# Recurrence gates from stacked high and low parts, and PSUM banks in rings of five and three

## The chip, the cores and the metric

The kernel runs on one core of one Trainium2 chip. The metric is the device time of one execution in microseconds, as the median of several runs. Below, PE is the matrix engine (TensorE), PEld its weight loads, DVE is VectorE, ACT is ScalarE, POOL is GpSimd and SP is the engine that issues most DMA transfers. A PE product writes into PSUM, which has eight banks; ACT and DVE read the results there.

## The reference, cut to what matters

The reference is one layer of a decoder that takes 1024 prompt tokens and 8 single tokens of other sequences, 1032 columns in all, through the same weights, in float32:

```python
z = x @ w_in                                     # one projection, 7680 columns for all branches
xr, yr, q, k, v, xq, g = split(z)
xc = conv4(xr);  a_out = rg_lru(xc) * gelu(yr)   # branch A
s_out = window_attention(q, k, v)                # branch B
c_out = memory_attention(xq, mem_k, mem_v)       # branch C
merged = sum(sigmoid(g[n] + b[n]) * (branch[n] @ w_branch[n]) for n in range(3))
h = layer_norm(ALPHA * x + merged @ w_out)
y = layer_norm(ALPHA * h + (silu(gate) * up) @ w_down)     # gate, up = split(h @ w_gate_up)
```

Inside `rg_lru` stand two small products, which the change is about. The 1024 channels are 16 blocks of 64, and each block has its own 64x64 matrix for each of two gates:

```python
r = sigmoid(einsum('btni,nij->btnj', xblk, wa) + ba)
i = sigmoid(einsum('btni,nij->btnj', xblk, wx) + bx)
log_a = -8 * r * softplus(-lam);  a = exp(log_a)
u = sqrt(-expm1(2 * log_a)) * (i * xf)           # then h = a * h + u along time
```

## The kernel before, in words

**Precision.** Each float32 operand is split into a high part, a cast to a shorter format made by ACT (L76), and a low part, the rest, made by a DVE subtraction (L77). A product is then three matmuls into one PSUM bank: high x high, high x low and low x high. `mm3` (L117 to L119) issues them.

**Recursive products.** Most large products are not multiplied block by block. `fast_step` computes a pair of 128-row output tiles ("a unit") from a 2x2 partition with seven products instead of eight, each from sums of quarters of the weights (`fast_quarter`) and of the input (`combos`, `h_combos`). A unit has seven steps, i = 0 to 6. Each step runs over two column halves, p = 0 and 1, of 258 columns, with twelve matmuls each (L237 to L239). Steps 0, 2, 4 and 6 add into one bank per half (`ub`), steps 1 and 5 into another (`ud`), step 3 has its own (`uc`). ACT copies the bank out after step 0 (`p1s`), step 1 (`p5s`) and step 2 (`u2s`), at L263; DVE reads it after step 3 (`za`, L265), step 4 (`zb`, L267) and step 5 (`za`, L270); ACT reads it after step 6 (`zb`, L1648). Within one bank the next step that adds must wait until the read before it is over: step 2 for p1s, step 4 for u2s, step 6 for zb of step 4. The quarters of the weights are cut three steps ahead.

**Stages.** `project` begins with the keys and values of the memory (`mem_kv`), then runs 30 units for the input projection. Behind each of its steps `pump` lets one side job issue a piece of work: the recurrence (`lru`) of a channel tile, the memory attention of the eight single tokens (`dec_mem`, whose dot products run on DVE from caches fetched by DMA, L895 and L901), or the transposed values. Then come the attentions, mixed with the branch products `bra`, `brc`, `brs`; the output projection; the gate and up products and most of the down products, again as recursive units (`gate_up_down`); and the last products (`dl`).

**Gates of the recurrence.** `lru(m)` works on tile m, that is 128 channels or two blocks of 64. The two 64x64 matrices of a gate stand on the diagonal of a 128x128 matrix that is otherwise zero, so `wr` is 128x256: gate a, then gate x. The columns are done in three thirds of 344. In each, xc is split into `xch` and `xcl`, and for each gate `mm3` makes three matmuls into the bank `g`, from which ACT writes the tanh of all 128 rows (L829) into `tr` (gate a) and `ti` (gate x). One piece of this is issued behind a step of the current unit.

**PSUM.** One pool of eight banks serves the whole kernel, in rings by use: `mm` 3, `s` 2, `t` 2, `o` 1. In `fast_step` the first sum takes from `mm`, the second from `t`, step 3 from `s`. The gates, the transposes of the single tokens (`drt_c`, `dct`) and the transposed values share the one bank of `o`.

**Order.** Up to the first six steps the order on every engine is as written. After that a scheduler places the instructions of each queue; PE keeps the order of the program but for small transposes, while ACT, DVE and SP get another order when costs or dependencies change. Each queue runs strictly in its order.

Of the kernel before, what the change touches and what calls it, by code (L numbers as in the profile page):

```python
# [10 lines left out]
F32 = mybir.dt.float32  # L11
# [7 lines left out]
P = 128  # L19
# [7 lines left out]
NM = 256  # L27
# [31 lines left out]
class Builder:  # L59
# [84 lines left out]
    def setup(self):  # L144
        nc, ctx, tc, io = self.nc, self.ctx, self.tc, self.io
        self.cst = ctx.enter_context(tc.tile_pool(name="cst", bufs=1))
        self.psum = ctx.enter_context(tc.tile_pool(name="psum", bufs=1, space=PSUM))
# [81 lines left out]
    def fast_product(self, st, i, p, ts, ps, opens):  # L229
# [5 lines left out]
        for k in range(4):  # L235
# [2 lines left out]
            mm(sh[:, w], xl, start=False, stop=False)  # L238
            self.last_mm = mm(sl[:, w], xh, start=False, stop=k == 3).ins  # L239

    def fast_step(self, st, i, ts, finish):

        nc, u, scale = self.nc, st["u"], getattr(finish, "scale", 1.0)
        cols = lambda th, p: slice(HT * th + QN * p, HT * th + QN * (p + 1))
        small = lambda tag, p: self.w1.tile([P, QN], F32, tag=tag, name=f"{tag}{u}_{p}", bufs=2)
        if i == 3:
            st["za"] = self.zt(f"za{u}")
        if i == 4:
            st["zb"] = self.zt(f"zb{u}")
        for p in range(2):  # L250
            if i == 0:
                st["b", p] = self.bank("mm", f"ub{u}_{p}")[:, :QN]
            elif i == 1:
                st["d", p] = self.bank("t", f"ud{u}_{p}")[:, :QN]
            elif i == 3:
                st["c", p] = self.bank("s", f"uc{u}_{p}")[:, :QN]
            b, c, d = st.get(("b", p)), st.get(("c", p)), st.get(("d", p))
            ps = {0: b, 1: d, 2: b, 3: c, 4: b, 5: d, 6: b}[i]
            self.fast_product(st, i, p, ts, ps, i in (0, 1, 3))
            add = partial(nc.vector.scalar_tensor_tensor, scalar=scale, op0=ALU.mult, op1=ALU.add)  # L260
            if i in (0, 1, 2):
                st["s", i, p] = small(("p1s", "p5s", "u2s")[i], p)
                self.last_copy = nc.scalar.mul(st["s", i, p], ps, scale).ins  # L263
            elif i == 3:
                add(st["za"][:, cols(0, p)], c, in1=st["s", 0, p])  # L265
            elif i == 4:
                self.last_evac = nc.vector.scalar_tensor_tensor(st["zb"][:, cols(1, p)], b, -scale, st["s", 1, p],  # L267
                                                                op0=ALU.mult, op1=ALU.subtract).ins
            elif i == 5:
                add(st["za"][:, cols(1, p)], d, in1=st["s", 2, p])  # L270
# [119 lines left out]
    def mem_kv(self, moving, xs, load, quarters):  # L390
# [7 lines left out]
        def put(ps, name, m):  # L398
            raw = self.ph.tile([P, 256], F32, tag="kvraw", name=f"{name}r{m}", bufs=4)
            nc.scalar.copy(raw, ps)  # L400
            nc.gpsimd.dma_start(self.scr[name][:, m, :], raw)

        def mem_raw(k):
# [20 lines left out]
        def key(n):  # L424
            m, e = n // 2, n % 2
            if e == 0:
                sums[m] = self.bank("mm", f"mk{m}")[:, :NM]
            hi, lo = pairs.pop(n)
            cols = [slice(i * P, (i + 1) * P) for i in range(4)]
            self.mm3(sums[m], [((hi[:, w], lo[:, w]), memx[4 * e + i]) for i, w in enumerate(cols)], e == 1, e == 0)  # L430

        def value(n):
            g, j = (n - 16) // 4, n % 4
            if j == 0:
                sums[g] = [self.bank("mm", f"mv{g}_{tt}")[:, :256] for tt in range(2)]
            hi, lo = pairs.pop(n)
            cols = [slice(i * 256, (i + 1) * 256) for i in range(2)]
            for tt in range(2):
                xs_ = [tuple(a[:, tt * P:(tt + 1) * P] for a in memx[2 * j + i]) for i in range(2)]
                self.mm3(sums[g][tt], [(x, (hi[:, w], lo[:, w])) for x, w in zip(xs_, cols)], j == 3, j == 0)  # L440

        warm = self.bank("o", "warm")
        for _ in range(WARM):
# [306 lines left out]
    def lru_consts(self):  # L750
# [9 lines left out]
        self.hbg = self.cst.tile([P, 24], F32, name="hbg")  # L760
        nc.vector.tensor_scalar_mul(self.hbg, self.vec[:, V_BG:V_BG + 24], 0.5)
# [38 lines left out]
    def lru(self, m, xr, yr):  # L800
# [15 lines left out]
        nc.gpsimd.tensor_copy(self.pconv[:, m, :], xr[:, TP - 3:TP])  # L816
        nc.gpsimd.tensor_copy(self.scvo[:, m, 0:2, :], buf[:, 1:3, :])
        nc.gpsimd.tensor_copy(self.scvo[:, m, 2, :], xr[:, TP:T])
        wgh, wgl = (self.lr.tile([P, 256], F32R, tag=f"wg{e}", name=f"wg{e}{m}", bufs=1) for e in "hl")
        self.split(wgh, wgl, wr)  # L820
        a, ti = self.zt(f"tr{m}"), self.zt(f"ti{m}")
        for c, (t0, n) in enumerate(THIRDS):
            xch, xcl = (self.lr.tile([P, n], F32R, tag=f"xc{e}", name=f"xc{e}{m}_{c}", bufs=1) for e in "hl")
            self.split(xch, xcl, xc[:, t0:t0 + n])
            yield
            for j, (dst, hb) in enumerate(((a, self.hba), (ti, self.hbx))):
                ps = self.bank("o", f"g{m}_{j}_{c}")[:, :n]
                self.mm3(ps, [((wgh[:, j * P:(j + 1) * P], wgl[:, j * P:(j + 1) * P]), (xch, xcl))])
                nc.scalar.activation(dst[:, t0:t0 + n], ps, AF.Tanh, bias=hb[:, m:m + 1], scale=0.5)  # L829
                yield  # L830

        sp2, sp4n = self.sp2[:, m:m + 1], self.sp4n[:, m:m + 1]
# [698 lines left out]
    def build(self):  # L1531
# [9 lines left out]
        self.wpool = self.ctx.enter_context(pool("wpool"))  # L1541
        self.ctx.enter_context(pool("edge", "right")).tile([P, 8], F32, name="edge")
        self.zbufs = 9
        with pool("tp", "right") as self.tp, pool("w1") as self.w1, pool("z") as self.z, ExitStack() as late:
            self.project(late, pool)
        self.act, self.merged, self.first_gates = {}, {}, []
        with ExitStack() as right:
            slots = right.enter_context(ExitStack())
# [36 lines left out]
            with pool("zf") as self.z:  # L1585
                with ExitStack() as tx:
                    self.g, self.wl, self.wraw, self.A = [], [], [], {}
                    with pool("lnp") as self.ph:
# [5 lines left out]
                    with pool("w1") as self.w1:  # L1594
# [94 lines left out]
def _pack(i):  # L1689
# [28 lines left out]
    blk = np.zeros((KT, P, 256), np.float32)  # L1718
    for j, name in enumerate(("lru_wa", "lru_wx")):
        w = f[name][0].reshape(KT, 2, 64, 64)  # L1720
        for e in range(2):
            blk[:, e * 64:(e + 1) * 64, j * P + e * 64:j * P + (e + 1) * 64] = w[:, e]
    o["wlru"] = blk
# [53 lines left out]
```

## Time and profile before

| | us |
|---|---|
| median of 3 runs | 1907.44 (1907.36 to 1909.93) |
| the profiled execution | 1909.41 |
| its span, first to last instruction | 1907.6 |
| PE busy in the span | 1889.4 |
| DVE busy | 1389.9 |
| ACT busy | 1014.8 |

The profile shows one execution. PE matmuls are pipelined: one starts while the one before still runs, so its busy time says that PE had work, and its rate is read from the spacing of starts. A row of a group gives line, engine, operation, what it writes and reads, how often; then the busy time, the mean duration in ns, the idle time before it, and what ended that. A row of the timeline gives start, duration, engine, line, operation. The chain of waits is followed back from the last instruction. The mean granted clock of PE was 0.997.

### The profile page before, as it was taken

What the parts mean: (1) busy time and instruction counts of PE and PEld (TensorE: products, weight loads), DVE (VectorE), ACT (ScalarE), POOL (GpSimd) and SP (SyncE); (2) the same over time, 40 slices, a digit from 0 to 9 for tenths busy, and PEclk for the clock granted to TensorE, in tenths of its full rate; (3) what the DMA queues carried; (4) which work ended last, traced back from release to release, by engine and by line L of the source; (5) the groups of instructions that cost most, each with busy time, mean ns of one, the idle gap of its engine ahead of it and who ended that gap; (6) DMA issues with size and microseconds to landing.
All of it is one profiled execution on the core that took longest, in us unless ns stands there. A gap on an engine that the chain in (4) does not pass through costs nothing.

```text
span 1907.6 us, 38153 instructions
## 1 busy us (share of the span) xinstructions
PE 1889.4 (99%) x14878; PEld 1870.0 (98%) x14878; DVE 1389.9 (73%) x2712; ACT 1014.8 (53%) x2124; POOL 112.8 (6%) x190
## 2 busy tenths in 40 slices
PE   9999999999999999999999999999999999999998
PEld 8999999999999999999999999999999999999997
DVE  7868877977887657578887467786666667858486
ACT  6555564555665656578775234543433433636354
POOL 1000000010000000022210000000000000001200
PEclk9999999999999999999999999999999999999998
DMA  8535434546444368546435351133355335759872
GB/s 316 171 119 173 136 128 139 172 144 214 136 150 147 113 209 264 181 144 208 144 100 164 111 190 51 57 122 118 111 165 191 106 123 177 269 127 272 174 211 90
DMA packets 175973, 302.18 MB, mean 158 GB/s; under 512 B 18912, under 2 KB 92592, under 8 KB 175792
## 3 DMA queue, kind: packets, MB, share of 16 engines
q1 hardware_dynamic: 169120, 280.64, 45.0%
q0 software_dynamic: 4224, 14.78, 3.9%
q10 hardware_dynamic: 2448, 4.33, 0.6%
q8 instruction: 116, 1.90, 0.4%
q14 instruction: 65, 0.53, 0.1%
HBM read 217.97 MB, written 85.89 MB: 159 GB/s over the span
## 4 chain that ended last, share of the span: by engine, by line
PE 90%; DMA 4%; DVE 3%; ACT 2%; issue 1%; SPq 0%; DVEq 0%; ACTq 0%
PE ub L237 5%; PE ub L239 5%; PE ub L238 5%; PE ubfg L238 4%; PE ubfg L237 4%; PE ubfg L239 4%; PE ud L239 3%; PE ud L237 3%; PE ud L238 3%; PE udfg L237 2%; PE udfg L238 2%; PE udfg L239 2%; PE ubf L237 2%; PE op L117 2%; PE ubf L238 2%; PE ubf L239 2%
## 5 line engine op out<-in xcount | busy, mean ns | idle before, releaser
L645 ACT ACTIVATE bp<-bp,bst 128x257 f32<-128x257 f32 (+1 forms) x128 | 62.8, 493 | 38.5 <-DVE bst L639 37.8
L237 PE MATMUL ub<-th,u_0h 128*128 128x258 f32 x240 | 68.6, 286 | 1.0 <-ACT zb L1648 1.0
L237 PE MATMUL ub<-th,u_6h 128*128 128x258 f32 x240 | 68.7, 286 | 0.0
L237 PE MATMUL ub<-th,u_4h 128*128 128x258 f32 x240 | 68.0, 283 | 0.7 <-ACT u2s L263 0.7
L237 PE MATMUL ub<-th,u_2h 128*128 128x258 f32 x240 | 68.0, 283 | 0.4 <-ACT p1s L263 0.4
L239 PE MATMUL ub<-th,u_0l 128*128 128x258 f32 x240 | 68.0, 283 | 0.0
L639 DVE CUSTOM_DVE_ANT_0 bp<-bs,mask,nsnk 128x256 f32<-128x256 f32 (+1 forms) x128 | 55.8, 461 | 16.8 <-PE bs L636 16.4
L239 PE MATMUL ud<-th,u_5l 128*128 128x258 f32 x240 | 68.0, 283 | 0.0
L237 PE MATMUL ud<-th,u_5h 128*128 128x258 f32 x240 | 67.9, 283 | 0.0
L239 PE MATMUL ud<-th,u_1l 128*128 128x258 f32 x240 | 67.9, 283 | 0.0
L239 PE MATMUL ub<-th,u_2l 128*128 128x258 f32 x240 | 67.9, 283 | 0.0
L239 PE MATMUL uc<-th,u_3l 128*128 128x258 f32 x240 | 67.9, 283 | 0.0
L239 PE MATMUL ub<-th,u_6l 128*128 128x258 f32 x240 | 67.9, 283 | 0.0
L239 PE MATMUL ub<-th,u_4l 128*128 128x258 f32 x240 | 67.9, 283 | 0.0
L237 PE MATMUL uc<-th,u_3h 128*128 128x258 f32 x240 | 67.9, 283 | 0.0
L237 PE MATMUL ud<-th,u_1h 128*128 128x258 f32 x240 | 67.9, 283 | 0.0
L238 PE MATMUL ub<-tl,u_0h 128*128 128x258 f32 x240 | 67.6, 282 | 0.0
L238 PE MATMUL ub<-tl,u_6h 128*128 128x258 f32 x240 | 67.5, 281 | 0.0
L238 PE MATMUL ub<-tl,u_2h 128*128 128x258 f32 x240 | 67.4, 281 | 0.0
L238 PE MATMUL uc<-tl,u_3h 128*128 128x258 f32 x240 | 67.4, 281 | 0.0
L238 PE MATMUL ud<-tl,u_5h 128*128 128x258 f32 x240 | 67.4, 281 | 0.0
L238 PE MATMUL ud<-tl,u_1h 128*128 128x258 f32 x240 | 67.4, 281 | 0.0
(949 smaller groups left out, 8294.8 us busy)
## 6 DMA issues: line engine op xcount, KB each, us to landing
ur<-win SPq DMA_DIRECT2D x120, 256.0 KB, 3.2
urfg<-wgu SPq DMA_DIRECT2D x80, 256.0 KB, 2.8
scr_f<-G SPq DMA_DIRECT2D x22, 516.0 KB, 3.1
f<-scr_f SPq DMA_DIRECT2D x16, 516.0 KB, 4.9
fs<-scr_t SPq DMA_DIRECT2D x16, 516.0 KB, 5.5
dck<-cmk SPq DMA_DIRECT2D x32, 256.0 KB, 4.1
dcv<-cmvT SPq DMA_DIRECT2D x32, 256.0 KB, 4.2
urf<-wdn SPq DMA_DIRECT2D x32, 256.0 KB, 2.9
```

The lines of the kernel that those rows point to most:

```text
L117: nc.tensor.matmul(ps, sh, mh, start=opens and i == 0, stop=False)
L237: mm(sh[:, w], xh, start=opens and k == 0, stop=False)
L238: mm(sh[:, w], xl, start=False, stop=False)
L239: self.last_mm = mm(sl[:, w], xh, start=False, stop=k == 3).ins
L639: nc.vector.tensor_tensor_reduce(pg[g], s[:, u * 256:u * 256 + n], msk, 1.0, snk[:, g:g + 1], ALU.add, ALU.min, st[:, g:g + 1])
L645: nc.scalar.activation(x, x, AF.Exp, bias=st[:, g:g + 1], scale=-1.0, accum_out=st[:, 4 + g:5 + g])
```

## The change

It has two parts.

**Stacked parts.** The gates go one block of 64 rows at a time. For block e, a tile `x[e]` of 128 rows holds the high part of the block's 64 channels in one half of its rows and their low part in the other. The weight matrix for block e repeats the same 64 rows in both halves, and has 64 columns for gate a and 64 for gate x. One matmul with the high weights then gives high x high plus high x low, and a second with the low weights gives low x high (and low x low); both gates of the block come out in one bank. Block 0 has its columns in the order a, x, block 1 in the order x, a, so that the gate-a rows of a block stand in their own half of the bank; those of gate x stand in the other half, and ACT moves them on its way out. So each third has two groups of two matmuls for two groups of three, four tanh of 64 rows for two of 128, and two casts and two subtractions of 64 rows for one of each of 128. `wlru` is packed anew on the host, in the same size, and the bias `hbx` is stored with its halves swapped by two ACT instructions in place of one on DVE.

**Banks.** During `project` and during `gate_up_down` five banks form a queue, `idle`: whoever needs a bank takes the oldest free one (`take`), and a unit gives back its second pair behind step 5 and its first pair behind step 6. Everything else in these stages (step 3, gates, transposes) turns through one ring of three. The eight banks are therefore four pools one after the other: `psum0` for `project`, `psum1` with the old rings up to the first feed-forward products, `psum2` for `gate_up_down`, `psum3` with the old rings for the end.

```diff
     def bank(self, tag, name):
+        if self.idle is not None:
+            return self.psum.tile([P, 512], F32, tag="s", name=name, bufs=3)
         return self.psum.tile([P, 512], F32, tag=tag, name=name, bufs=BANKS[tag])
+
+    def take(self, name):
+        k = self.idle.popleft()
+        return k, self.psum.tile([P, 512], F32, tag=f"x{k}", name=name, bufs=1)
...
+    def sum_bank(self, st, tag, name):
+        if self.idle is None:
+            return self.bank(tag, name)[:, :QN]
+        k, ps = self.take(name)
+        st.setdefault("banks", []).append(k)
+        return ps[:, :QN]
...
             if i == 0:
-                st["b", p] = self.bank("mm", f"ub{u}_{p}")[:, :QN]
+                st["b", p] = self.sum_bank(st, "mm", f"ub{u}_{p}")
             elif i == 1:
-                st["d", p] = self.bank("t", f"ud{u}_{p}")[:, :QN]
+                st["d", p] = self.sum_bank(st, "t", f"ud{u}_{p}")
...
+        if self.idle is not None and i > 4:
+            self.idle += st["banks"][2:] if i == 5 else st["banks"][:2]
...
-        nc.vector.tensor_scalar_mul(self.hbx, self.vec[:, V_BX:V_BX + 8], 0.5)
+        for r in (0, 64):
+            nc.scalar.mul(self.hbx[r:r + 64], self.vec[64 - r:P - r, V_BX:V_BX + 8], 0.5)
...
-        wgh, wgl = (self.lr.tile([P, 256], F32R, tag=f"wg{e}", name=f"wg{e}{m}", bufs=1) for e in "hl")
-        self.split(wgh, wgl, wr)
+        wg = tuple(self.lr.tile([P, 256], F32R, tag=f"wg{e}", name=f"wg{e}{m}", bufs=1) for e in "hl")
+        half = [slice(e * 64, e * 64 + 64) for e in range(2)]
+        self.split(*wg, wr)
...
-            xch, xcl = (self.lr.tile([P, n], F32R, tag=f"xc{e}", name=f"xc{e}{m}_{c}", bufs=1) for e in "hl")
-            self.split(xch, xcl, xc[:, t0:t0 + n])
+            x = [self.lr.tile([P, n], F32R, tag=f"xc{e}", name=f"xc{e}{m}_{c}", bufs=1) for e in range(2)]
+            for e, r in enumerate(half):
+                src = xc[r, t0:t0 + n]
+                nc.scalar.copy(x[e][r], src)
+                nc.vector.tensor_sub(x[e][half[1 - e]], src, x[e][r].bitcast(F32))
             yield
-            for j, (dst, hb) in enumerate(((a, self.hba), (ti, self.hbx))):
-                ps = self.bank("o", f"g{m}_{j}_{c}")[:, :n]
-                self.mm3(ps, [((wgh[:, j * P:(j + 1) * P], wgl[:, j * P:(j + 1) * P]), (xch, xcl))])
-                nc.scalar.activation(dst[:, t0:t0 + n], ps, AF.Tanh, bias=hb[:, m:m + 1], scale=0.5)
+            for e in range(2):
+                ps = self.bank("o", f"g{m}_{e}_{c}")[:, :n]
+                for i in range(2):
+                    nc.tensor.matmul(ps, wg[i][:, e * P:(e + 1) * P], x[e], start=i == 0, stop=i == 1)
+                for dst, hb, f in ((a, self.hba, half[e]), (ti, self.hbx, half[1 - e])):
+                    nc.scalar.activation(dst[half[e], t0:t0 + n], ps[f], AF.Tanh, bias=hb[f, m:m + 1], scale=0.5)
                 yield
...
+        banks = lambda name: tc.tile_pool(name=name, bufs=1, space=PSUM, reuse_waits="tile")
...
+            with banks("psum0") as self.psum:
+                self.idle = deque(range(5))
+                self.project(late, pool)
+        self.idle, psum = None, ExitStack()
+        self.psum = psum.enter_context(banks("psum1"))
...
+                    psum.close()
+                    with pool("w1") as self.w1, banks("psum2") as self.psum:
+                        self.idle = deque(range(5))
                         self.gate_up_down(ts)
+                    self.idle, self.psum = None, self.ctx.enter_context(banks("psum3"))
```

The scheduler also moves instructions. On ACT, at the first tile's first thirds, the queue stood so before (`tr` and `ti` are the tanh of the gates, `xch` the cast of the next third, `u_.h` casts of weights):

```order
L829 ACTIVATE tr_1621<-g_0_0_1666,lruc 128x344
L76 CAST u_2h<-us_2_1751 128x512
L829 ACTIVATE ti_1622<-g_1_0_1702,lruc 128x344
L76 CAST xch_1_1747<-xc_1486 128x344
L76 CAST u_3h<-ur_01_1536 128x512
L1654 ACTIVATE za_1637<-za_1637,hbg 128x1032
L1648 ACTIVATE zb_1675<-ub_0_1494 128x258
L76 CAST u_4h<-us_4_1845 128x512
L1648 ACTIVATE zb_1675<-ub_1_1509 128x258
```

and stands so now:

```order
L852 ACTIVATE tr_1622<-g_0_0_1669,lruc 64x344
L852 ACTIVATE ti_1623<-g_0_0_1669,lruc 64x344
L844 CAST xc_1_1750<-xc_1487 64x344
L82 CAST u_2h<-us_2_1756 128x512
L852 ACTIVATE tr_1622<-g_1_0_1705,lruc 64x344
L852 ACTIVATE ti_1623<-g_1_0_1705,lruc 64x344
L844 CAST xc_1_1751<-xc_1487 64x344
L82 CAST u_3h<-ur_01_1537 128x512
L1685 ACTIVATE za_1640<-za_1640,hbg 128x1032
L1679 ACTIVATE zb_1678<-ub_0_1495 128x258
L82 CAST u_4h<-us_4_1850 128x512
L1679 ACTIVATE zb_1678<-ub_1_1510 128x258
```

Ahead of each of the two casts of weights stand two tanh and a cast of 64 rows.

On DVE, at the same place, the queue stood so before (`za` and `zb` read the banks of steps 3 and 4, `xcl` is the low part of the second third, `u_.l` low parts of weights):

```order
L265 SCALAR_TENSOR_TENSOR za_1637<-uc_1_1652,p1s_1_1522 128x258
L77 TENSOR_TENSOR u_0l<-ur_00_1534,u_0h 128x512
L267 SCALAR_TENSOR_TENSOR zb_1675<-ub_0_1494,p5s_0_1561 128x258
L267 SCALAR_TENSOR_TENSOR zb_1675<-ub_1_1509,p5s_1_1576 128x258
L77 TENSOR_TENSOR u_1l<-us_1_1715,u_1h 128x512
L221 TENSOR_TENSOR us_5_1891<-us_2_1751,ur_01_1536 128x512
L77 TENSOR_TENSOR xcl_1_1748<-xc_1486,xch_1_1747 128x344
```

and stands so now:

```order
L278 SCALAR_TENSOR_TENSOR za_1640<-uc_1_1655,p1s_1_1523 128x258
L83 TENSOR_TENSOR u_0l<-ur_00_1535,u_0h 128x512
L845 TENSOR_TENSOR xc_1_1750<-xc_1487,xc_1_1750 64x344
L280 SCALAR_TENSOR_TENSOR zb_1678<-ub_0_1495,p5s_0_1562 128x258
L280 SCALAR_TENSOR_TENSOR zb_1678<-ub_1_1510,p5s_1_1577 128x258
L83 TENSOR_TENSOR u_1l<-us_1_1718,u_1h 128x512
L226 TENSOR_TENSOR us_5_1898<-us_2_1756,ur_01_1537 128x512
L845 TENSOR_TENSOR xc_1_1751<-xc_1487,xc_1_1751 64x344
```

One of the two subtractions of the third now stands ahead of the two reads of step 4.

On PE the order is the same but for the dropped matmuls and small transposes. What an instruction waits for differs by its bank. At step 0 of the third unit, where the second column half begins, PE's queue had before (in brackets the engine waited for):

```order
L237 MATMUL ub_0_1494<-th_0_122,u_0h 128x258
L238 MATMUL ub_0_1494<-tl_0_123,u_0h 128x258
L239 MATMUL ub_0_1494<-th_0_122,u_0l 128x258
L237 MATMUL ub_1_1509<-th_1_124,u_0h 128x258 [waits Activation_49]
L238 MATMUL ub_1_1509<-tl_1_125,u_0h 128x258
```

and has now:

```order
L242 MATMUL ub_0_1495<-th_0_122,u_0h 128x258
L243 MATMUL ub_0_1495<-tl_0_123,u_0h 128x258
L244 MATMUL ub_0_1495<-th_0_122,u_0l 128x258
L242 MATMUL ub_1_1510<-th_1_124,u_0h 128x258 [waits DVE_49]
L243 MATMUL ub_1_1510<-tl_1_125,u_0h 128x258
```

The second half waited for a read of its bank by ACT, and now waits for one by DVE.

More of the change, by code (lines that the diff above doesn't have):

```diff
@@ L396, in mem_kv, with put @@
         order = [(f, p) for f in ((0, 0), (0, 1), (1, 1), (1, 0)) for p in range(2)]
-        def put(ps, name, m):
+        def put(bank, name, m):
             raw = self.ph.tile([P, 256], F32, tag="kvraw", name=f"{name}r{m}", bufs=4)
-            nc.scalar.copy(raw, ps)
+            nc.scalar.copy(raw, bank[1][:, :256])
+            self.idle.append(bank[0])
             nc.gpsimd.dma_start(self.scr[name][:, m, :], raw)
@@ L426, in key @@
             if e == 0:
-                sums[m] = self.bank("mm", f"mk{m}")[:, :NM]
+                sums[m] = self.take(f"mk{m}")
             hi, lo = pairs.pop(n)
             cols = [slice(i * P, (i + 1) * P) for i in range(4)]
-            self.mm3(sums[m], [((hi[:, w], lo[:, w]), memx[4 * e + i]) for i, w in enumerate(cols)], e == 1, e == 0)
+            self.mm3(sums[m][1][:, :NM], [((hi[:, w], lo[:, w]), memx[4 * e + i]) for i, w in enumerate(cols)], e == 1, e == 0)
         def value(n):
@@ L434, in value @@
             if j == 0:
-                sums[g] = [self.bank("mm", f"mv{g}_{tt}")[:, :256] for tt in range(2)]
+                sums[g] = [self.take(f"mv{g}_{tt}") for tt in range(2)]
             hi, lo = pairs.pop(n)
@@ L439, in value @@
                 xs_ = [tuple(a[:, tt * P:(tt + 1) * P] for a in memx[2 * j + i]) for i in range(2)]
-                self.mm3(sums[g][tt], [(x, (hi[:, w], lo[:, w])) for x, w in zip(xs_, cols)], j == 3, j == 0)
+                self.mm3(sums[g][tt][1][:, :256], [(x, (hi[:, w], lo[:, w])) for x, w in zip(xs_, cols)], j == 3, j == 0)
         warm = self.bank("o", "warm")
@@ L1717, in _pack @@
     o["wdn"] = mtiles(f["w_down"][0])
-    blk = np.zeros((KT, P, 256), np.float32)
+    blk = np.zeros((KT, 2, 64, 2, P), np.float32)
     for j, name in enumerate(("lru_wa", "lru_wx")):
```

8 lines of the change are left out of this document (3 added, 5 removed).

## The prediction

> **What bounds the kernel now.** The page comes first: who is busy, and which engine the chain of waits runs over.
>
> ```profile
> PE 1889.4 (99%) x14878; PEld 1870.0 (98%) x14878; DVE 1389.9 (73%) x2712; ACT 1014.8 (53%) x2124; POOL 112.8 (6%) x190
> PE 90%; DMA 4%; DVE 3%; ACT 2%; issue 1%; SPq 0%; DVEq 0%; ACTq 0%
> ```
>
> TensorE (PE) is busy 99% of the span and carries 90% of the chain. That share is a mean over stages, so the next view is the busy time by stretches: the end of the combinations, the stage with the recurrence, and the gate, up and down products.
>
> ```profile
> 55.00:105.00 50.00, 48.22 (x398) 47.62 (x397) 42.61 (x108) 25.05 (x52) 4.16 (x12) 1.00 0.52 160
> 105.00:640.00 535.00, 534.36 (x4405) 532.68 (x4404) 420.72 (x847) 315.29 (x597) 31.35 (x37) 1.00 0.46 148
> 1300.00:1825.00 525.00, 524.91 (x4362) 524.70 (x4361) 350.93 (x539) 232.23 (x453) 19.08 (x22) 1.00 0.57 172
> ```
>
> The columns are length, then busy time of PE, weight load, DVE, ACT and POOL, granted clock, DMA. Between 105 and 640 us, where all gate products of the recurrence stand, PE lacks 0.6 us of 535; DVE works 79% of it and ACT 59%. Between 1300 and 1825 us PE lacks 0.1 us. The third view is what PE waited for in the first two stretches (total, times, longest; the first two rows are of 105 to 640 us).
>
> ```profile
> PE ub L237 <- ACT p1s L263: 0.4, 1, 0.4
> PE dct L921 <- ACT ti L829: 0.2, 1, 0.2
> PE ub L237 <- ACT zb L1648: 1.0, 1, 1.0
> PE ub L237 <- ACT u2s L263: 0.7, 1, 0.7
> ```
>
> So in the changed stages PE is the bound by its own work. An instruction taken from PE shortens the run by its spacing, unless a new wait takes its place; and better PSUM rings have at most the rows above to win.
>
> **The gate products.** They lie between the recursive products, and their price is the spacing of starts, not the duration, since matmuls overlap.
>
> ```profile
> 111.63 0.28 PE L239 MATMUL uc<-th,u_3l 128*128 128x258 f32 x1
> 111.75 0.32 PE L117 MATMUL g<-xch,wgh 128*128 128x344 f32 x1
> 111.90 0.32 PE L118 MATMUL g<-xcl,wgh 128*128 128x344 f32 x1
> 112.06 0.32 PE L119 MATMUL g<-xch,wgl 128*128 128x344 f32 x1
> 112.22 0.28 PE L237 MATMUL ub<-th,u_4h 128*128 128x258 f32 x1
> ...
> L118 PE MATMUL g<-xcl,wgh 128*128 128x344 f32 x48 | 15.3, 319 | 0.0
> ```
>
> Three gate products take 112.22 - 111.75 = 0.47 us, 0.157 each; a product of 258 columns takes 0.12 (111.63 to 111.75). Each third of each of the eight channel tiles has two groups of three: 24 x 2 x 3 = 144. Stacking leaves two per group, 96. The 48 that go, as many as the row of L118 counts, are worth 48 x 0.157 = 7.5 us. The weights they used are loaded all the same, once fewer per group.
>
> [...]
>
> **What ACT and DVE get in return.** A third had one cast, one subtraction and two tanh of 128 rows. Now it has two casts, two subtractions and four tanh of 64 rows. Whether 64 rows cost half is read from pairs of the same length:
>
> ```profile
> L829 ACT ACTIVATE tr<-g,lruc 128x344 f32<-128x344 f32 x24 | 13.0, 544 | 0.0
> L76 ACT CAST xch<-xc 128x344 fp32r<-128x344 f32 x24 | 11.5, 477 | 12.3 <-DVE xc L813 12.3
> L676 ACT COPY bob<-bo 64x512 f32<-64x512 f32 x32 | 18.7, 583 | 11.3 <-PE bo L674 10.7
> L543 ACT COPY cob<-co 128x512 f32<-128x512 f32 x16 | 9.4, 585 | 10.0 <-PE co L119 7.8 <-DMA scr_c<-cob 2.2
> L77 DVE TENSOR_TENSOR xcl<-xc,xch 128x344 fp32r<-128x344 f32 x24 | 12.4, 516 | 8.5 <-ACT xch L76 8.1
> L677 DVE TENSOR_TENSOR bob<-bo,bob 64x512 f32<-64x512 f32 x32 | 21.8, 681 | 7.6 <-ACT bob L676 7.1
> L77 DVE TENSOR_TENSOR bpl<-bt,bph 128x512 fp32r<-128x512 f32 x60 | 41.1, 687 | 7.6 <-ACT bph L76 7.1
> ```
>
> They do not: 583 ns against 585 on ACT, 681 against 687 on DVE. So a third adds 2 x 0.544 + 0.477 = 1.57 us to ACT and 0.516 to DVE, in all 24 x 1.57 = 38 us and 12.4 us. ACT goes from 315 to 353 of 535 us (66%), DVE from 421 to 433 (81%). What hides them is the products between a value's making and its use. The tightest such link is DVE's: step 6 adds to the bank that DVE reads as zb after step 4, with 36 products, 36 x 0.12 = 4.3 us, between. Here it was used up:
>
> ```profile
> 415.79 0.42 DVE L267 SCALAR_TENSOR_TENSOR zb<-ub,p5s 128x258 f32<-128x258 f32 x1
> 416.13 0.28 PE L239 MATMUL ud<-th,u_5l 128*128 128x258 f32 x1
> 416.27 0.39 PE L237 MATMUL ub<-th,u_6h 128*128 128x258 f32 x1
> ```
>
> zb ends at 416.21 and PE goes on at 416.27, 0.02 us late. Such places can come to cost what the third adds. Bounds: below, nothing, since a moved queue can also come out better (the 0.4 us behind p1s may go); above, one tanh for each third, 24 x 0.544 = 13.1 us. The stage's listed waits are 0.6 us while DVE is already at 79%; two points more are near that, so I take twice as much, 1.2 us. Behind a late zb on DVE stand the low halves of the next weights; behind a late cast on ACT stand p1s and u2s, which step 2 and step 4 wait for.
>
> **The rings.** After the change the two sums of a unit take their four banks from a queue of five, and the products of step 3, the gates and the small transposes turn through three. The one wait of 1.0 us was for a bank:
>
> ```profile
> 99.99 1.25 ACT L809 ACTIVATE xc<-za,vec 128x1032 f32<-128x1032 f32 x1 [3.19 <-DVE za L270]
> 101.15 0.36 ACT L1648 ACTIVATE zb<-ub 128x258 f32<-128x258 f32 x1
> ...
> 100.25 0.28 PE L239 MATMUL ub<-th,u_0l 128*128 128x258 f32 x1
> 101.56 0.39 PE L237 MATMUL ub<-th,u_0h 128*128 128x258 f32 x1 [1.04 <-ACT zb L1648]
> ```
>
> At step 0 of the third unit its second column half got the bank that ACT was still reading, behind 1.25 us of convolution. The spacing there is 1.31 us instead of 0.12, so 1.2 us are lost. In the new order this product waits for DVE instead: its bank is that of the unit before's second sum, read a step earlier. ACT's read is next needed two column halves later, 2 x 12 x 0.12 = 2.9 us after 100.25, and it ends at 101.51. I take the 1.2 us, and the 0.2 us of the transpose that stood behind ti, as gone. In the first projections nothing waits for a bank in these rows, and between 1300 and 1825 us 0.1 us is all there is to win. The joints between the four new sets of banks must not cost either. In the built program the nearest is the last one: the second group of the last products gets the bank of the last column half.
>
> ```profile
> 1824.80 0.63 ACT L1629 ACTIVATE zbf<-ubf 128x258 f32<-128x258 f32 x2
> 1826.09 0.29 PE L117 MATMUL dl<-g5h,wl0h 128*128 128x258 f32 x1
> ```
>
> ACT leaves it at 1825.43, and the group starts at 1826.09: 0.66 us of cover, so nothing; if ACT came 1 us later, 0.3 us. The SP queue keeps its weight loads in order, with loads of the decode attention moved by a place or two; ACT's two new bias rows of 64 partitions are a few tenths of a microsecond once.
>
> **The sum.** -7.5 - 1.2 - 0.2 + 1.2 = -7.7 us. The profiled execution took 1909.4 us for its span of 1907.6, so 1901.7 of its own kind; it is 2.0 us above the median of the three runs, 1907.44, and against that median the forecast is 1899.7 us.
>
> **The rivals.** First: the rings give nothing, or the shared three take back what the five give, since a bank of the gates is now let go only after two tanh, 2 x 0.544 us. For it: the products of step 3 used to have two banks to themselves. Against it: the gate products had one bank before, and no row shows a wait for it except the 0.2 us. Time: 1907.44 - 7.5 + 1.2 = 1901.1.
>
> Second: DVE pays more than the count. Its small instructions overlap today:
>
> ```profile
> 71.29 0.16 DVE L759 TENSOR_SCALAR nsnk<-vec 128x16 f32<-128x16 f32 x1
> 71.37 0.17 DVE L761 TENSOR_SCALAR hbg<-vec 128x24 f32<-128x24 f32 x1
> ```
>
> The second starts 0.08 us before the first is over. The subtractions now read one half of the partitions and write the other. If that stops the overlap at three joints of a pair, a third adds 0.516 + 3 x 0.08 = 0.76 us to DVE, and if once in each of the eight tiles zb is late by all of it, 8 x 0.76 = 6.1 us come back: 1907.44 - 8.9 + 6.1 = 1904.6. For it: the cover was used up at 416.21, and the stage has DVE at 79%. Against it: 21% are free, and PE lost only 0.6 us there. [...]
>
> Third, the other side: ACT becomes the bound in the thirds. PE gains 2 x 0.157 = 0.31 us in a third, and ACT gets 1.57. From the point at which PE waits more than 0.31 us in a mean third, the change loses. One tanh ahead of p1s or u2s in each, fully exposed, gives 24 x 0.544 = 13.1 us: 1907.44 - 8.9 + 13.1 = 1911.6. For it: PE waited for p1s and u2s, 0.4 and 0.7 us. Against it: ACT has 41% to itself in this stage and catches up within a step or two.
>
> **How the numbers follow.** Forecast 0.72, first rival 0.10, second 0.12, third 0.06. A difference of under 0.2%, 3.8 us, can't be told from none. The first two are faster by more (1899.7 and 1901.1 against 1903.6), the second rival within, the third slower: 0.82, 0.12, 0.06. The forecast's own range goes from 1897.5 (no new wait, and the 0.4 and 0.7 us gone too: 1907.44 - 8.9 - 1.1) to 1903.5 (5 us of new waits). The range runs on to 1906.0, over the second rival, and leaves out the third.
>
> **What would show it.** Between 105 and 640 us the same work should end 8 us earlier; gate matmuls should count 96, still 0.157 us apart; the row for zb L1648 at 100 us should be gone, as should the transpose behind ti. ACT should show 96 tanh and 48 casts of 64 rows at the old means, and DVE 48 subtractions at about 516 ns. New rows of PE waiting for zb, p1s, u2s or a gate's bank should total 1 to 2 us. The stretch that was 1300 to 1825 us should be as long as before. Waits of PE for DVE in the thirds of over 4 us speak for the second rival; rows of p1s or u2s with 24 or more waits for the third. The forecast is wrong if the 48 products are gone and the stage is not shorter by more than 4 us.

## The result and the profile after

The changed kernel takes 1904.81 us (median of 17 runs, 1901.92 to 1907.23) against 1908.19 us for the kernel before (17 runs, 1906.92 to 1911.17): ratio 0.998, 95% interval 0.9973 to 0.9987, or 3.4 us less. The forecast was 7.7 us less. The profiled execution took 1906.67 us for a span of 1904.8.

First the page of the changed kernel, then its busy time by stretches (length, then PE, weight load, DVE, ACT, POOL, granted clock, DMA):

```profile
PE 1881.9 (99%) x14830; PEld 1862.8 (98%) x14830; DVE 1402.2 (74%) x2735; ACT 1055.5 (55%) x2198; POOL 108.6 (6%) x190
...
105.00:640.00 535.00, 533.57 (x4409) 532.71 (x4409) 436.90 (x878) 358.27 (x674) 28.56 (x38) 1.00 0.45 149
1300.00:1825.00 525.00, 523.68 (x4351) 523.46 (x4351) 352.10 (x549) 234.89 (x463) 20.85 (x24) 1.00 0.57 173
```

PE has 48 matmuls fewer and 7.5 us less busy time, DVE 12.3 us more, ACT 40.7 us more. PE now lacks 1.4 us of 535 in the first stretch (0.6 before) and 1.3 us in the second (0.1 before).

Next, where the time went. The rows give the first and last start of a product, before and after: the first branch product (end of the recurrence stage), the memory scores, the window products, the last products.

```profile
L117 PE MATMUL bra<-baH,wba_h x192: 278/337/447, 692.5 to 870.6; 128*128 128x384 f32 x64, 128*128 128x390 f32 x64, 128*128 128x258 f32 x64
L117 PE MATMUL cs<-mkh,cqh x64: 274/283/287, 715.2 to 778.2; 128*128 128x256 f32 x64
L674 PE MATMUL bo<-bpl,vs x60: 389/394/496, 805.6 to 1013.8; 128*128 128x512 f32 x60
L117 PE MATMUL dl<-g5h,wl0h x16: 277/282/287, 1823.9 to 1880.1; 128*128 128x258 f32 x16
```
```profile
L123 PE MATMUL bra<-baH,wba_h x192: 277/336/444, 684.8 to 866.4; 128*128 128x384 f32 x64, 128*128 128x390 f32 x64, 128*128 128x258 f32 x64
L123 PE MATMUL cs<-mkh,cqh x64: 277/283/385, 707.4 to 772.5; 128*128 128x256 f32 x64
L690 PE MATMUL bo<-bpl,vs x60: 389/394/505, 801.4 to 1009.9; 128*128 128x512 f32 x60
L123 PE MATMUL dl<-g5h,wl0h x16: 277/282/358, 1821.6 to 1877.9; 128*128 128x258 f32 x16
```

At the end of the recurrence stage PE is 692.5 - 684.8 = 7.7 us ahead, and so it is at the first score (7.8). At the last window product it is 3.9 us ahead: 3.9 us are lost in the attentions, where nothing of the source was changed. At the first last product it is 2.3 us ahead, 1.5 us lost in one place, since the last recursive product was still 3.8 us ahead. The end comes 2.8 us earlier. The gain that was forecast came, and about 5 us of it were given back later.

The largest waits of PE that are new or longer than before (total, times, longest; whole program):

```profile
PE dl L123 <- ACT zbf L1660: 1.3, 1, 1.3
PE co L124 <- DVE cpl L83: 1.8, 4, 0.6
PE co L123 <- ACT cob L559: 1.2, 1, 1.2
PE ub L242 <- DVE zb L280: 1.3, 1, 1.3
```

`dl` stands at the joint to the last products; `co` are the products of probabilities and values in the memory attention (their waits for `cpl` were 0.7 us before); the last row is in the recurrence stage.

### The profile page after: what moved, and what is told of

Same layout as the page of the kernel before. It is cut to its first block, busy times and chain, and to the rows that moved or that the text cites. A ratio compares the mean times of both kernels' runs of the same rounds, so it can differ in the third digit from the quotient of the medians.

```text
span 1904.8 us, 38214 instructions
## 1 busy us (share of the span) xinstructions
PE 1881.9 (99%) x14830; PEld 1862.8 (98%) x14830; DVE 1402.2 (74%) x2735; ACT 1055.5 (55%) x2198; POOL 108.6 (6%) x190
## 4 chain that ended last, share of the span: by engine, by line
PE 90%; DMA 4%; DVE 3%; ACT 2%; issue 1%; SPq 0%; DVEq 0%; ACTq 0%
PE ub L244 6%; PE ub L242 6%; PE ub L243 6%; PE ubfg L243 4%; PE ubfg L244 4%; PE ubfg L242 4%; PE ud L244 3%; PE ud L243 3%; PE ud L242 3%; PE udfg L244 2%; PE udfg L242 2%; PE udfg L243 2%; PE op L123 2%; PE op L125 2%; PE op L124 2%; PE brs L123 2%
## 5 line engine op out<-in xcount | busy, mean ns | idle before, releaser
L243 PE MATMUL ub<-tl,u_4h 128*128 128x258 f32 x240 | 67.6, 282 | 0.0
```

## The experiments

Theory A: the gates and rings gave what was forecast; what was given back comes from two places. At the last joint the first group of the last products has a bank that VectorE reads late. In the memory attention the new pools led the scheduler to another order on ACT, DVE and SP. Against it stand B (the ACT and DVE work that 64-row blocks add makes the later stages longer), C (transfers that differ from run to run) and D (the joint waits for ACT, as the row above says). Theories E and F came later. Times below are medians, ratios against the kernel before on the same chip.

**The gates alone.** The kernel before with the diff's parts in `lru`, `hbx` and `wlru`; pool and rings as before.

> The kernel before with the stacked gates alone; the PSUM pool and its rings stay as before, and the order of ScalarE, VectorE and SyncE from the attention on is that of the kernel before. Theory A (the gates gave what was forecast, the rest of the change gives part of it back): TensorE 6.3 to 7.5 us earlier at the end of the recurrence stage, the memory attention and the joint before the last products as long as before, so 1900.7 to 1901.9 us. Rival B (the ScalarE and VectorE work that the 64-row blocks add is what makes the later stages longer): about as the changed kernel, 1904 to 1905 us.

Measured: 1906.16 us, ratio 0.9986 (0.9977 to 0.9995), 2.4 us less. The joint has no wait (the first `dl` starts 0.1 us after the last recursive product). But PE is only 4.6 us ahead at the first branch product, 3.1 us short of the changed kernel. Its waits from 105 to 694 us say why in part:

```profile
PE ub L237 <- DVE zb L267: 1.4, 1, 1.4
PE g L834 <- ACT ti L836: 1.1, 1, 1.1
PE drt_c L879 <- ACT ti L836: 0.4, 1, 0.4
...
PE dct L928 <- ACT ti L836: 0.3, 1, 0.3
```

1.8 us are waits for `ti`: the one bank of ring `o` is now let go only after two tanh. So theory A had the gates alone too good, and the time lies above B's range as well. A was also wrong on the attention, which lost 2 us here though the queues of ACT and DVE stand as before; the last values waited for a store (see the end of this section).

**The rings alone.** The changed kernel with `lru`, `hbx` and `wlru` of before.

> The changed kernel with the gates of the kernel before: new PSUM pools and rings, no stacked gates. In the memory attention ScalarE, VectorE and SyncE have the order of the changed kernel. Theory A: gains 1.2 to 1.4 us in the first stages (the bank wait near 100 us), loses 3.5 us in the memory attention and 1.5 us at the joint before the last products, so slower than before by 3 to 4 us, 1911 to 1912 us. Rival B (the added gate work makes the loss): 1 us faster than before or the same, 1907 to 1908 us.

Measured: 1912.72 us, ratio 1.0023 (1.0014 to 1.0032), 4.1 us more. The kernel has none of the added gate work, and still its joint waits 1.5 us and the stretch from the first score to the last window product (714.4 to 1016.9) is 3.9 us longer than before. B falls as the cause of these two losses: the pools alone make both. At the first branch product they had gained 1.1 us (691.4).

**The order of before in the memory attention.** ORDER lists the positions in which ACT, DVE and SP issued the instructions of that stage in the kernel before; each is queued behind the one before it.

```diff
+        start = len(nc.cur_bb.bb.instructions)
...
+            traced = nc.cur_bb.bb.instructions[start:]
+            for run in ORDER:
+                for k, j in zip(run, run[1:]):
+                    self.behind(traced[j], traced[k])
```

> The changed kernel with the order of ScalarE, VectorE and SyncE in the memory attention set to that of the kernel before (queue order alone, no wait added); gates, banks and all other places as in the changed kernel. Theory A (the loss of 3.5 us between the first scores and the last values of the memory attention comes from the order of the queues): that stretch is as long as before, 5.0 us at most apart from 0.5, so about 1901.3 us; the joint before the last products still loses 1.5 us. Rival C (the loss is of transfers that come at another time, or differs from run to run, whatever the order): as the changed kernel, 1904 to 1905 us.

Measured: 1904.16 us, ratio 0.9976 (0.9967 to 0.9985). By the time this is rival C's range and not A's 1901.3 us: the median is only 0.7 us under the changed kernel, which the intervals can't tell from none. In the trace, as A has it, the stretch from the first score to the last product of values is 709.3 to 788.8, 79.5 us (before 79.3, changed kernel 82.9). Its profiled run had a granted clock of 0.996, that of the changed kernel 0.998; what that does to the length of its stages was not shown, so they are not compared to a microsecond. One turn of the attention shows the mechanism. `cph` and `cpl` are the two halves of the turned probabilities, made in pairs; `cqh` and `cql` those of the next queries. In the changed kernel:

```profile
727.15 0.59 ACT L82 CAST cph<-cpt 128x512 fp32r<-128x512 f32 x1
729.03 1.05 ACT L82 CAST cqh<-cql 128x1024 fp32r<-128x1024 f32 x1 [1.30 <-DMA cql<-scr_xq]
729.99 0.58 ACT L82 CAST cph<-cpt 128x512 fp32r<-128x512 f32 x1
730.11 1.22 DVE L83 TENSOR_TENSOR cql<-cql,cqh 128x1024 fp32r<-128x1024 f32 x1 [1.66 <-ACT cqh L82]
731.26 0.68 DVE L83 TENSOR_TENSOR cpl<-cpt,cph 128x512 fp32r<-128x512 f32 x1
732.00 0.50 PE L124 MATMUL co<-cpl,mv 128*128 128x512 f32 x1 [0.52 <-DVE cpl L83]
```

and with the order of before:

```profile
728.54 0.60 ACT L82 CAST cph<-cpt 128x512 fp32r<-128x512 f32 x1
729.05 0.59 ACT L82 CAST cph<-cpt 128x512 fp32r<-128x512 f32 x1
729.54 1.05 ACT L82 CAST cqh<-cql 128x1024 fp32r<-128x1024 f32 x1
...
729.17 1.29 DVE L83 TENSOR_TENSOR cpl<-cpt,cph 128x512 fp32r<-128x512 f32 x2
```

The changed order puts the cast of the next queries between the two casts of probabilities. ACT stands 1.30 us at its head, for a transfer that has not landed. The second cast comes behind it, DVE's second subtraction behind that of the queries, and PE waits for it. Over the eight turns ACT stands 5.3 to 7.5 us for these transfers in the five traces with the changed order, and 2.6 to 3.7 us in the six with the order of before. In the built program SP too issues four of these eight loads one to three places later in the changed order. The run sets all three queues back at once, so their shares are not separated.

**The new rings in the project stage only.** The changed kernel with one old-style pool from the attention to the end.

```diff
-                    psum.close()
-                    with pool("w1") as self.w1, banks("psum2") as self.psum:
-                        self.idle = deque(range(5))
+                    with pool("w1") as self.w1:
                         self.gate_up_down(ts)
-                    self.idle, self.psum = None, self.ctx.enter_context(banks("psum3"))
```

> The changed kernel with the rings of five and three in the project stage only; from the attention on one PSUM pool with the old rings to the end, so that the first last product has a bank that nobody holds. The memory attention has the order of the changed kernel. Theory A (TensorE waits at the joint for VectorE's read of the first group's bank behind six weight subtractions): the 1.5 us wait goes, the last product begins 0.1 us after the last recursive product, the loss of 3.5 us in the attention stays: about 1903.3 us. Rival D (the joint waits for ScalarE's copy or for an operand, as the trace names it, whichever bank it is): the wait stays, 1904 to 1905 us.

Measured: 1902.11 us, ratio 0.9969 (0.9956 to 0.9981), 6.5 us less and 3 us under the changed kernel, of which the joint explains half. These are 5 runs with an interval of 2.4 us either way; whether the rest is more than that, the trace does not show. In it the joint's 1.5 us are gone and the attention's loss remains (first score to last window product 302.0 us, before 298.6, changed kernel 302.5). In the built program the first last product has here a bank that was free; in the changed kernel it has the bank of step 5's first half. That D is wrong a row of the run with the order of before says outright, where ACT's copy came later than DVE's sum:

```profile
1819.87 0.75 DVE L283 SCALAR_TENSOR_TENSOR zaf<-udf,u2sf 128x258 f32<-128x258 f32 x2
1820.35 0.64 ACT L1678 ACTIVATE zbf<-ubf 128x258 f32<-128x258 f32 x2
1820.43 0.36 PE L123 MATMUL dl<-g5h,wl0h 128*128 128x258 f32 x1 [1.31 <-DVE zaf L283]
```

PE starts 0.08 us after ACT has begun its two copies, which take 0.64 us. In the changed kernel DVE's sums and ACT's copies start within 0.1 us, and the trace's view puts the wait down to ACT. There DVE comes so late because six subtractions for the next weights stand ahead:

```profile
1819.48 1.66 DVE L1410 SCALAR_TENSOR_TENSOR wl0l<-wl1r,wbar,wl0h 128x128 fp32r<-128x128 f32 x6
1821.06 0.75 DVE L283 SCALAR_TENSOR_TENSOR zaf<-udf,u2sf 128x258 f32<-128x258 f32 x2
1821.14 0.63 ACT L1660 ACTIVATE zbf<-ubf 128x258 f32<-128x258 f32 x2
```

**The changed kernel again, and both repairs.** The first of these three is the changed kernel itself; the second joins the two edits above; the third has the order of before, all four pools, and at the joint (`subs` holds the six subtractions):

```diff
-                add(st["za"][:, cols(1, p)], d, in1=st["s", 2, p])
+                self.last_za = add(st["za"][:, cols(1, p)], d, in1=st["s", 2, p]).ins
...
                         self.gate_up_down(ts)
+                    for ins in self.subs:
+                        self.behind(ins, self.last_za)
```

> The changed kernel once more, beside the next two on one chip. Theory A (the order of the queues makes the memory attention longer): its stretch from the first score to the last product of values is again 82.9 us give or take 0.8, and the joint before the last products again 1.6 us; 1904.2 to 1905.2 us. Rival C (what the transfers do differs from run to run): the stretch may come out anywhere between 79.4 and 83 us.

> Both repairs together: the new rings in the project stage only, and the order of ScalarE, VectorE and SyncE in the memory attention set to that of the kernel before. Theory A: stretch of the memory attention 79.4 to 80.0 us, no wait at the joint, and the time 1 to 3 us below that of the rings in the project stage alone (1902.1 us), 1899.1 to 1901.1 us. Rival C: stretch and time as with the rings in the project stage alone, 82.6 us and 1901.5 to 1902.7 us.

> The changed kernel with the memory attention in the order of before and, at the last joint, VectorE's two sums out of the first group's banks queued ahead of its six weight subtractions; all PSUM pools as in the changed kernel. Theory A (TensorE waits there for VectorE's read of the first group's bank): the wait of 1.5 us falls to 0 to 0.5 us though bank and copy by ScalarE stay as they are; 1.0 to 1.5 us below the same kernel without that step (1904.2 us), 1902.7 to 1903.2 us. Rival D (it waits for ScalarE's copy of the second group's bank): the wait stays at 1.5 us, 1904.2 us.

Measured: the changed kernel 1905.77 us, ratio 0.9985 (0.9976 to 0.9993); both repairs 1901.36 us, 0.9962 (0.9948 to 0.9976); the sums first 1902.29 us, 0.9966 (0.9954 to 0.9979). The joint of the changed kernel lost 1.5 us again, but its attention (first score to last value product) took 81.2 us, outside the 82.9 give or take 0.8 that A expected, and its time is 0.6 us above A's range: the order's cost varies, so C is right in part. With the two sums ahead, the wait at the joint is gone with banks and pools as they were:

```profile
1816.12 0.75 DVE L283 SCALAR_TENSOR_TENSOR zaf<-udf,u2sf 128x258 f32<-128x258 f32 x2
1816.78 0.28 PE L123 MATMUL dl<-g5h,wl0h 128*128 128x258 f32 x1
```

The last recursive product starts at 1816.66, and ACT's copies begin only at 1818.07: D is out. Both repairs give 7.1 us less than before, the lowest median of all versions, but only 0.7 us less than the rings in the project stage alone, where 1 to 3 were expected; the intervals of these two overlap.

**The sums first, without the order.** The same edit at the joint on the changed kernel.

> The changed kernel with VectorE's two sums queued ahead of its six weight subtractions at the last joint, and nothing else: the memory attention has the order of the changed kernel. With the changed kernel, the order of before alone and both steps it makes a table of two by two. Theory A: no wait at the joint, the memory attention 2 to 4 us longer than before from its first score to the last product of the window attention; 1.0 to 1.9 us below the changed kernel (1904.8 and 1905.8 us) and 1 to 3 us above the one with both steps (1902.3 us): 1903.3 to 1904.5 us. Rival C (the order does not matter, transfers differ from run to run): as with both steps, 1902 to 1902.6 us.

Measured: 1904.20 us, ratio 0.9976 (0.9967 to 0.9985). The time is in A's range. The traced execution is the slowest of the 11 (1907.87 us), and in it PE still lost 0.8 us at the joint. The sums stand ahead of the six subtractions now, but two of `g7l`, the low half of an operand of the last products, stand ahead of the sums and came later here, after a wait for ACT:

```profile
1819.46 2.53 DVE L83 TENSOR_TENSOR g7l<-g7l,g7h 128x1032 fp32r<-128x1032 f32 x2 [0.67 <-ACT g7h L82]
1821.91 0.75 DVE L283 SCALAR_TENSOR_TENSOR zaf<-udf,u2sf 128x258 f32<-128x258 f32 x2
```

Two by two, as differences from the kernel before:

| | order as changed | order of before |
|---|---|---|
| joint as changed | -3.4 and -2.7 | -4.4 |
| sums first | -4.5 | -6.1 |

By the medians each step is worth 1 to 1.8 us, and nothing speaks against adding them. But each entry has an interval of 1.3 to 2.4 us either way, so no single difference is shown by the times; the traces tell the steps apart better. The time from the first to the last start of the score product row (`cs`), in all profiled kernels:

| order of ACT, DVE, SP | us |
|---|---|
| of before: before, gates alone, order of before, both repairs, sums first with it, gates in two rings | 63.0, 63.8, 63.2, 63.6, 63.0, 63.8 |
| as changed: changed twice, rings alone, rings in project, sums first without it | 65.1, 64.5, 65.7, 65.3, 66.7 |

No run of one kind lies among the other. The order costs 0.7 to 3.7 us there. Over the longer stretch, from the first score to the last window product, the kinds meet: 298.6 to 300.7 us with the order of before, 300.7 to 303.4 as changed. The kernels that differ in the order alone stay apart there too (302.5 and 300.7 to 299.0; 302.0 to 299.2; 303.4 to 298.6). By the times the order costs 1.0 to 1.7 us in the table of two by two, and 0.7 us between the rings in the project stage with and without it.

**Gates in two rings.** In the kernel with the gates alone, the two groups of a third take banks from `o` and `s`:

```diff
-                ps = self.bank("o", f"g{m}_{e}_{c}")[:, :n]
+                ps = self.bank("os"[e], f"g{m}_{e}_{c}")[:, :n]
```

> The stacked gates alone on the old PSUM pool, as in the run of the gates alone, but the two column halves take their banks from two rings (the one bank of ring o, and ring s) instead of both from the one bank of ring o. Order of the attention as in the kernel before. Theory E (with the old rings the stacked gates lose 2.1 us to waits for the one bank, which ScalarE reads twice a group): the waits of the gates and of the transposes for the tanh fall from 2.1 us to under 0.5 us, TensorE is 6.3 to 7.0 us earlier at the end of the recurrence stage instead of 4.7, and the time is 1.5 to 2.2 us below that of the gates alone (1906.2 us): 1904.0 to 1904.7 us. Rival F (what is missing there comes of the added work on ScalarE and VectorE, whichever bank): as the gates alone, or the waits move to the sums of the recursive products that share ring s: 1905.5 to 1907 us.

Measured: 1905.37 us, ratio 0.9988 (0.9979 to 0.9997). PE is 5.4 us ahead at the first branch product (687.1) instead of 4.6, where E expected 6.3 to 7.0; by the times the run can't be told from the gates alone. The waits from 105 to 694 us, beside the 1.4 us for DVE's `zb`:

```profile
PE ub L237 <- ACT zb L1655: 1.3, 3, 0.6
PE uc L237 <- ACT ti L836: 0.5, 2, 0.2
```

The waits of gates and transposes for `ti` are gone, as E has it, and as F has it most of that moved: the products of step 3 wait for `ti` in the shared ring, and first sums wait for ACT's `zb` a second and third time. With five and three (the last row of the waits of the changed kernel) only `zb` L280 is left.

**Not settled.** The last product of values waits for ACT's copy, whose buffer is still being stored, in four of the five traces with the changed order and in one of the six with the order of before. In the changed kernel this is 1.2 of the 3.9 us that the attentions lost. In the run of the gates alone:

```profile
789.53 0.58 ACT L543 COPY cob<-co 128x512 f32<-128x512 f32 x1 [1.48 <-DMA scr_c<-cob]
790.16 0.49 PE L117 MATMUL co<-cph,mv 128*128 128x512 f32 x1 [1.04 <-ACT cob L543]
...
DMA to landing us min/median/max: 5.3/6.8/7.9
```

The stores there took up to 7.9 us to land, and up to 6.9 us in the run with the order of before, where PE did not wait for them. Between 778 and 790 us the transfers move 353 GB/s in the first of these runs, 374 in the second and 277 in the kernel before. That the loads of the next stage slow the stores is argued, not shown; a third buffer was not tried.

## Why the prediction was wrong

**The gate products were right.** There are 96 gate matmuls, and their spacing is as before:

```profile
110.33 0.32 PE L850 MATMUL g<-xc,wgh 128*128 128x344 f32 x1
110.49 0.32 PE L850 MATMUL g<-xc,wgl 128*128 128x344 f32 x1
110.65 0.28 PE L242 MATMUL ub<-th,u_4h 128*128 128x258 f32 x1
```

0.16 us each. The stage ends 7.7 us earlier, against the sum's 7.7 at that place. That 64 rows cost what 128 do is right too for these instructions (543 ns against 544 for a tanh, 511 against 516 for a subtraction), with ACT 40.7 us up (38 forecast) and DVE 12.3 (12.4):

```profile
L852 ACT ACTIVATE ti<-g,lruc 64x344 f32<-64x344 f32 x48 | 26.1, 543 | 0.8
L845 DVE TENSOR_TENSOR xc<-xc,xc 64x344 fp32r<-64x344 f32 x48 | 24.5, 511 | 16.4 <-ACT xc L844 15.5
```

**The new waits were right in size and place, not in cause.** One wait of 1.3 us for 1.2, of step 6 for `zb`, at the unit that the prediction quoted. The prediction put it to the added work of the gates. But the rings alone, without that work, have a wait of 0.9 us at the same place, and the stacked kernels have 1.1 to 2.0 us. DVE was not short of time there. It stood 2.51 us for a transfer of the single tokens' attention, and then a long instruction came ahead of `zb`:

```profile
408.90 0.42 DVE L924 SCALAR_TENSOR_TENSOR dcj<-dcv,dcvq 128x256 f32<-128x256 f32 x1 [2.51 <-DMA dcv<-cmvT]
409.25 1.23 DVE L864 SCALAR_TENSOR_TENSOR th<-tr,th 128x1032 f32<-128x1032 f32 x1
410.40 0.75 DVE L280 SCALAR_TENSOR_TENSOR zb<-ub,p5s 128x258 f32<-128x258 f32 x2
```
```profile
410.87 0.39 PE L242 MATMUL ub<-th,u_6h 128*128 128x258 f32 x1 [1.32 <-DVE zb L280]
```

In the kernel before DVE stood 1.86 us for such a transfer at this place, and `zb` came 0.02 us late for PE. So the term's size came right by luck.

**The rings were right in sum, wrong in parts.** The 1.2 us behind ACT's `zb` at 100 us are gone, but they go with the gates alone as well as with the rings alone. The ground given against the first rival, that one bank had served the gates without a wait, does not hold for gates that are read twice: alone they gain 4.6 us at the end of the stage, the rings alone 1.1, both 7.7. So 2 us exist only together. (With the rings alone the first projection product started 0.8 us later than before, at 58.0 us; counted from that product the gains are 4.2, 1.9 and 7.5 us, and 1.4 us exist only together.)

**First failing step: "the nearest is the last one: the second group of the last products gets the bank of the last column half".** The nearest was the first group. It got a bank of step 5, one that DVE, not ACT, lets go, 1.66 us of subtractions later. The price given for a late ACT, 0.3 us, was for the wrong reader. In the four traces with this joint as the change has it (the changed kernel twice, the rings alone, the order of before) PE lost 1.5 us each time; by the times it is 1.1 to 1.8 us.

**Second failing step: "The SP queue keeps its weight loads in order, with loads of the decode attention moved by a place or two".** The prediction looked for moved instructions only where the source had changed; the order of ACT and DVE in the memory attention has no term in it. There 20 places of ACT's queue, 44 of DVE's and 17 of SP's hold another instruction than before, in the built program, without a changed line. It costs 0.7 to 1.7 us by the times and up to 3.7 us in a trace.

With both put back the ratio is 0.9962 (0.9948 to 0.9976), or 0.9966 (0.9954 to 0.9979) with the rings of `gate_up_down` kept, and the forecast's own, 1899.7 / 1907.44 = 0.9959, lies within both. The mechanism of the gain was right; the sum lacked these two terms. By the times they make 1.8 to 3.5 us of the 4.3 that are missing (7.7 - 3.4); the rest is within the intervals.

**The rivals and the range.** The first (rings give nothing) is out by the gates alone: without the rings 3.1 us of the stage's 7.7 are missing. The third (ACT becomes the bound) is out: no new rows for p1s or u2s. The second has its mechanism and not its price. A row of DVE before and after:

```profile
116.95 0.51 DVE L77 TENSOR_TENSOR xcl<-xc,xch 128x344 fp32r<-128x344 f32 x1
117.38 0.42 DVE L270 SCALAR_TENSOR_TENSOR za<-ud,u2s 128x258 f32<-128x258 f32 x1
```
```profile
112.71 0.68 DVE L83 TENSOR_TENSOR u_0l<-ur,u_0h 128x512 fp32r<-128x512 f32 x1
113.42 0.51 DVE L845 TENSOR_TENSOR xc<-xc,xc 64x344 fp32r<-64x344 f32 x1
113.96 0.43 DVE L280 SCALAR_TENSOR_TENSOR zb<-ub,p5s 128x258 f32<-128x258 f32 x1
```

Before, the next instruction started 0.08 us before the subtraction's end; now it starts 0.03 us after it, and so does the subtraction after the one ahead of it. So a joint costs 0.11 us here, not 0.08. In the trace of the changed kernel no DVE instruction starts before such a subtraction ahead of it is over, and behind 40 of the 48 the next starts within 0.01 to 0.03 us of the end; in that of the kernel before it starts 0.04 to 0.10 us before the end behind 17 of the 24. Why the overlap goes no run shows. PE did not wait for it: of the stage's waits only the `zb` above is DVE's, 1.3 us where this rival has 6.1. So it is luck that the measured 1904.81 us lies beside its 1904.6, and with that inside the stated range: what was lost was lost in later stages, which neither the forecast nor a rival had priced. (The range's lower end adds up to 1897.4, not 1897.5; nothing hangs on it.)

## What to carry to other kernels

A change can pay in full where it is made and be given back where no line was touched: when a scheduler orders the queues, compare the order of every engine in every stage, and ask of each instruction that can wait for a transfer what now stands behind it. Where one set of banks follows another, look up the reader of the bank that the very first product gets, and what is queued ahead of that reader. A stacked operand that is read out in more pieces can hold its bank longer, here through two tanh of 0.54 us in place of one, and the gates alone paid 1.8 us of waits for that; so matmuls saved and banks to turn through belong to one change.

## What the runs showed of the hardware that was not expected

One kind of transfer took from 2.0 to 8.1 us to land in one execution. The stores of `cob`, 256 KB each, in the changed kernel from 710 to 780 us and from 778 to 792 us (minimum, median and maximum from issue to landing):

```profile
DMA to landing us min/median/max: 2.0/3.7/4.5
...
DMA to landing us min/median/max: 5.6/6.9/8.1
```

So a buffer that was free in time in one run was late in another: at the last value product PE waited 1.04 us in the run of the gates alone, and not at all in that with the order of before. And a queue that had such a wait ahead of other work passed it on: ACT stood 1.30 us for the next queries, and PE 0.52 us for the second half of the probabilities behind them.
